# Writing each weight's low part in two halves: a one-core kernel for a hybrid decoder layer

## The chip, the core and the metric

The kernel runs on one core of one Trainium2 chip. The metric is the device time of one execution in microseconds (us). The core has a matrix engine (PE; its weight loads are shown as PEld), a vector engine (DVE), an activation engine (ACT), a general engine (POOL) and an engine that only issues transfers (SP). Each works through its own queue of instructions in order and waits for the others by semaphores.

## What is computed

One layer of a decoder, for a prompt of 1024 tokens and a sample group of 8 x 8 tokens with the same weights. Two branches read the same input: A, sparse attention, whose keys are the best 256 by a small indexer; B, gated linear attention (GLA) over four heads. Cut to what matters here:

```python
z = split_projection(x @ w_in)                 # q, k, v, indexer, GLA and gate columns
attn = attend(q_a, k_a, v_a, q_i, k_i, z['w_i'])      # top 256 keys by indexer score, softmax
log_a = log_sigmoid(z['a_b'] @ w_alpha2 + b_alpha) / GATE_TAU
o_b, s_new = gla_chunked(q_b, k_b, v_b, log_a, s0, chunk)
...
branch_a = attn @ w_attn_o
branch_b = o_b @ w_gla_o
merged = sigmoid(z['gate_a']) * branch_a + sigmoid(z['gate_b']) * branch_b
h = layer_norm(DN_ALPHA * x + merged @ w_out, ln1_g, ln1_b)
ff = square(relu(h @ w_ff1)) @ w_ff2
y = layer_norm(DN_ALPHA * h + ff, ln2_g, ln2_b)
```

## The kernel before

The 1024 prompt tokens and 64 sample tokens stand side by side as 1088 columns, cut into chunks of 384, 384 and 320. Products are taken in single precision out of two reduced parts: an operand is the sum of a high part (`h`, a rounding copy on ACT) and a low part (`l`, the rest, a subtraction), and `mm3` makes three matmuls of each product: high by high, high by low, low by high.

The program has two phases. `front` holds the projections, the GLA, the indexer with its search for the 256 best keys, the attention, the merge and the output projection; `back` holds the MLP and the sample group's attention. In `front` the list `jobs` gives the order in which the weights are used: indexer queries, keys and values, attention queries, then for each GLA head its query, key and value weights, and between these the `g` and gate weights, last the three output weights of the branches. Each job has one weight of 128 output columns, 8 x 128 rows, so a page of 128 x 1024; the value weights of the GLA (`wvb`) have 256 columns and take two pages, and those of `wao` are 128 x 512.

For a weight, `w_load` (L493) issues the transfer into a raw page `wr`. `w_split` (L504) takes the pages `wh` and `wl`, writes the high part on ACT and makes a task of the low part. `w_low` (L515) is that task: it waits until `wh` is there by the planner's estimate, then writes `wl = wr - wh` by `sub` (L443). `sub` puts it on POOL or DVE, whichever the planner thinks will be done first, with a bonus for POOL (`WLATE`, 4 us, in all but the first and the last jobs). `w_get` (L528), called when a job begins, splits the next job's weight and runs what is left of its own weight's tasks at once. The first two weights are split by other code at the start.

What sets the order of instructions is a planner that runs while the program is written. `Clock` keeps an estimated time for each engine and for each written range of a tile. The streams (`Stream`, generators that write instructions and yield what they need next) stand in a list in `Order`; `run` (L309) takes the first one in the list whose needs are met by the estimate at PE's present time, lets it write up to its next yield, and begins again at the head of the list. Tasks stand at the head, then the attention, the GLA, the searches, and at the end the main stream with the projections, which fills PE when nothing else is ready. A stream that yields an empty tuple is ready again at once. So any change in what is written, or in its estimated time, can move instructions of all streams on all engines.

The names of the prediction: `qz` casts and `qi` subtractions on DVE come from the indexer's queries, `psi` are its score matmuls and `sc` its accumulated scores; `ga`, `gb` and `jk`, `jkb` belong to two searches over the prompt's scores (bit by bit: a count, a comparison, a predicated copy, the next trial value), one counting on DVE and one on ACT; `ppr` is a small matmul of the search over the samples' scores. In the GLA, `S` is the state after a chunk, `Sm` the state scaled for the next chunk's matmul into `po`, `u` the scaled update out of `pu`, `gst` the samples' states and `us` their updates, `gv` the values, overwritten by the outputs.

## Time and profile before

| | |
|---|---|
| three runs | 2011.14, 2012.15, 2012.97 us (median 2012.15) |
| profiled execution, its own time | 2010.23 us |
| its span, first to last instruction | 2008.5 us |
| mean granted clock of PE | 0.996 |
| `wl` on POOL | 66 operations, 151.1 us, 2292 ns each |
| `wh` on ACT | 76 operations, 75.2 us, 997 ns each |
| PE waits up to 1060 us, longest | 2.6, 2.6, 2.4 and 1.8 us |
| moved by DMA | 260.30 MB, 130 GB/s |

The phase `front` takes PE until about 1060 us (the last `pwo` matmul with a `wl` starts at 1057.9), `back` the rest. A row of a group in the profile gives the line, the engine, the operation, what is written and read, the count, then the busy time and the mean of one in ns, then the idle time of the engine just before them and what ended it. Nearly every row has line L266, since a helper records each instruction; the names of the tiles tell them apart. A row of the timeline begins with the start and the length in us; what stands in brackets is the idle time just before it and what ended that. `x4` behind a row means four instructions in a row merged, and the length is then that of all four.

### The profile page before, as it was taken

To read this page: it belongs to the slowest core of one execution; us is meant where nothing else is said; L and a number is where in the kernel's file an instruction comes from. 1 tells how busy PE (TensorE), PEld (TensorE's weight loads), DVE (VectorE), ACT (ScalarE), POOL (GpSimd) and SP (SyncE) were. 2 spreads that over 40 slices of the span, in tenths; PEclk is the share of its full clock that TensorE was granted. 3 is DMA by queue.
4 is the path that set the end of the run, shared out by engine and by line. 5 is a ranking of instruction groups with operands and counts; after the bars stand their busy time and mean duration, and the time that the engine had idled before them with its cause. 6 is when DMAs were issued, how large, how long until landed. Compare 5 with 4: busy or idle time off the path is not lost.

```text
span 2008.5 us, 34410 instructions
## 1 busy us (share of the span) xinstructions
PE 1978.6 (99%) x12341; PEld 1914.4 (95%) x12341; DVE 1294.2 (64%) x2698; ACT 1140.2 (57%) x2239; POOL 762.2 (38%) x569
## 2 busy tenths in 40 slices
PE   9999999999999999999999999999999999999998
PEld 8888989998999999999999999999999999999998
DVE  7886978887655856661376557777674445576635
ACT  6688768796667556770124445555654333445544
POOL 5143232232411132122133325656565543454455
PEclk9999999999999999999999999999999999999998
DMA  9464302213132234273761144555452354145542
GB/s 330 187 210 133 129 22 85 81 32 115 38 107 84 77 105 138 76 225 130 255 216 53 54 122 144 151 158 160 131 173 79 96 163 142 48 150 162 185 151 90
DMA packets 185163, 260.30 MB, mean 130 GB/s; under 512 B 22160, under 2 KB 121488, under 8 KB 184992
## 3 DMA queue, kind: packets, MB, share of 16 engines
q1 hardware_dynamic: 177440, 232.67, 36.4%
q0 software_dynamic: 7552, 25.43, 4.2%
q8 instruction: 97, 1.59, 0.3%
q14 instruction: 74, 0.61, 0.1%
HBM read 208.52 MB, written 49.51 MB: 128 GB/s over the span
## 4 chain that ended last, share of the span: by engine, by line
PE 64%; DVE 3%; issue 2%; ACT 1%; POOL 1%; SPq 1%; DMA 0%; ACTq 0%; POOLq 0%; DVEq 0%
PE pf L266 33%; PE gate L266 8%; PE pmb L266 5%; PE pwo L266 4%; PE pma L266 2%; PE gb L266 2%; PE psq L266 2%; PE pov L266 2%; PE ppt L266 1%; PE pob L266 1%; PE psc L266 1%; DVE as L266 1%; PE pst L266 1%; SPq L266 1%; DVE w L266 0%
## 5 line engine op out<-in xcount | busy, mean ns | idle before, releaser
L266 PE MATMUL pf<-a,w 128*128 128x384 f32 (+1 forms) x2304 | 398.9, 329 | 3.2 <-POOL a L266 1.3
L266 PE MATMUL pf<-h,w 128*128 128x384 f32 (+1 forms) x2304 | 395.3, 329 | 0.0
L266 PEld LDWEIGHTS pf<-a,w 128*128 128x128 f32 x2304 | 379.7, 188 | 7.7 <-ACT a L266 2.1
L266 PEld LDWEIGHTS pf<-h,w 128*128 128x128 f32 x2304 | 380.4, 188 | 2.9
L266 POOL TENSOR_TENSOR wl<-wr,wh 128x1024 fp32r<-128x1024 f32 (+1 forms) x66 | 151.1, 2292 | 424.0 <-ACT wh L266 341.9
L266 POOL TENSOR_TENSOR w<-wr,w 128x512 fp32r<-128x512 f32 x135 | 191.4, 1426 | 128.5 <-ACT w L266 119.2
L266 ACT ACTIVATE w<-wr 128x512 fp32r<-128x512 f32 x256 | 148.0, 619 | 34.2 <-PE pf L266 18.4
L266 DVE TENSOR_TENSOR w<-wr,w 128x512 fp32r<-128x512 f32 x121 | 123.1, 1023 | 53.0 <-ACT w L266 51.6
L266 DVE TENSOR_TENSOR acc<-acc,pf 128x384 f32<-128x384 f32 (+1 forms) x152 | 81.3, 538 | 82.5 <-PE pf L266 81.9
L266 PE MATMUL gate<-xh,wh 128*128 128x384 f32 (+1 forms) x384 | 130.2, 339 | 0.0
L266 PE MATMUL gate<-xh,wl 128*128 128x384 f32 (+1 forms) x384 | 125.5, 327 | 0.0
L266 PE MATMUL gate<-xl,wh 128*128 128x384 f32 (+1 forms) x384 | 125.4, 327 | 0.0
L266 ACT ACTIVATE wh<-wr 128x1024 fp32r<-128x1024 f32 (+1 forms) x76 | 75.2, 997 | 82.7 <-PE pmb L266 57.9
L266 POOL TENSOR_TENSOR a<-fr,a 128x384 fp32r<-128x384 f32 (+1 forms) x52 | 50.7, 975 | 181.7 <-ACT a L266 179.0
L266 ACT ACTIVATE a<-fr 128x384 fp32r<-128x384 f32 (+1 forms) x96 | 48.7, 507 | 105.7 <-DVE fr L266 104.3
L266 DVE TENSOR_TENSOR fr<-fr,pf 128x384 f32<-128x384 f32 (+1 forms) x96 | 50.7, 529 | 72.7 <-ACT fr L266 72.1
L266 ACT ACTIVATE jkb<-sc,gb_f 128x896 int8<-128x896 f32 (+2 forms) x96 | 86.1, 897 | 19.9 <-DVE gb_f L266 17.3
L266 ACT ACTIVATE fr<-pf 128x384 f32<-128x384 f32 (+1 forms) x96 | 44.7, 465 | 81.2 <-PE pf L266 80.1
L266 DVE TENSOR_SCALAR_CACHE_REDUCE jk<-sc,ga_f 128x1024 int8<-128x1024 f32 (+2 forms) x96 | 88.4, 921 | 2.2
L266 DVE CUSTOM_DVE_ANT_0 pp<-psq,msk 128x512 f32<-128x512 f32 (+3 forms) x96 | 51.2, 553 | 47.8 <-PE psq L266 44.6
L266 PE MATMUL psv<-wh,xh 128*128 128x256 f32 x288 | 80.8, 285 | 0.0
L266 PE MATMUL psv<-wl,xh 128*128 128x256 f32 x288 | 80.3, 283 | 0.0
(532 smaller groups left out, 5138.3 us busy)
## 6 DMA issues: line engine op xcount, KB each, us to landing
wr<-wff SPq DMA_DIRECT2D x254, 256.0 KB
wr<-w SPq DMA_DIRECT2D x42, 512.0 KB
ckr<-kT SPq DMA_DIRECT2D x256, 64.0 KB
ga_s<-gate SPq DMA_DIRECT2D x16, 544.0 KB
ci_s<-cig SPq DMA_DIRECT2D x16, 512.0 KB
kir<-ci_s SPq DMA_DIRECT2D x16, 512.0 KB
mgp<-ga_s SPq DMA_DIRECT2D x16, 384.0 KB
qa_s<-qa SPq DMA_DIRECT2D x8, 544.0 KB
```

What stands on the lines that cost most here:

```text
L266: r = f(*a, **k)
```

## The change

`w_low` writes the low part by two operations, each of half the page's columns (the second dimension is the row tile, so a half is four of eight tiles, or two of four), and yields an empty tuple behind each, so that the planner looks for another stream between them. Engine and bonus are chosen for each half by itself; the bonus is computed once for both.

```diff
     def w_low(l, r, h):
         yield [f32(h)]
-        sub(l, r, f32(h), WLATE if 1 < state["job"] < mix_at - 1 else 0.0)
+        late = WLATE if 1 < state["job"] < mix_at - 1 else 0.0
+        m = r.shape[1] // 2
+        for s in (slice(0, m), slice(m, 2 * m)):
+            sub(l[:, s], r[:, s], f32(h[:, s]), late)
+            yield ()
```

The numbers of instructions change little beside this: POOL has 135 `wl` operations where it had 66, DVE 14 where it had 10 (three of the start in both), and a few evictions and scalings change between ACT and DVE. For 64 of the 73 weight pages both halves are on POOL, next to each other in its queue; for seven one half is on POOL and one on DVE, for two both on DVE. The matmuls are the same in number; their order changes between the indexer's scores and about the end of the gates, and from the merge of branch B on it is as before.

The queue of POOL in the first GLA head, before and with the change (`gat` a masked attention block, `gkz` the samples' keys, the two `wl` in a row a `wvb` weight's pages):

```order
L266 AFFINE_SELECT gat<-gat 128x512
L266 TENSOR_TENSOR wl_0_3057<-wr_0_2747,wh_0_3056 128x1024
L266 TENSOR_TENSOR gkz<-kts,brow 128x512
L266 AFFINE_SELECT gat<-gat 128x512
L266 TENSOR_TENSOR wl_0_3312<-wr_0_3052,wh_0_3311 128x1024
L266 TENSOR_TENSOR wl_1_3315<-wr_4_3054,wh_1_3314 128x1024
L266 TENSOR_TENSOR gkz<-kts,brow 128x512
```

```order
L266 AFFINE_SELECT gat<-gat 128x512
L266 TENSOR_TENSOR wl_0_3074<-wr_0_2768,wh_0_3073 128x512 x2
L266 TENSOR_TENSOR gkz<-kts,brow 128x512
L266 AFFINE_SELECT gat<-gat 128x512
L266 TENSOR_TENSOR wl_0_3340<-wr_0_3069,wh_0_3339 128x512 x2
L266 TENSOR_TENSOR wl_1_3343<-wr_4_3071,wh_1_3342 128x512 x2
L266 TENSOR_TENSOR gkz<-kts,brow 128x512
```

Each page's low part is now two operations side by side; the rest stands as it was.

The queue of DVE in the indexer's scores, where the prediction's place A is, before and with the change:

```order
L266 SCALAR_TENSOR_TENSOR sc_557<-r,wtok,sc_557 128x384
L266 SCALAR_TENSOR_TENSOR sc_556<-r,wtok,sc_556 128x512 x2
L266 CAST qz<-qi_568 64x4x8 x4
L266 SCALAR_TENSOR_TENSOR sc_559<-r,wtok,sc_559 128x384
L266 TENSOR_TENSOR qi_832<-qi_0_834,qi_832 64x384
L266 TENSOR_TENSOR qi_833<-qi_0_834,qi_833 64x384
L266 SCALAR_TENSOR_TENSOR sc_560<-r,wtok,sc_560 128x512
```

```order
L266 SCALAR_TENSOR_TENSOR sc_558<-r,wtok,sc_558 128x384
L266 SCALAR_TENSOR_TENSOR sc_557<-r,wtok,sc_557 128x512 x2
L266 TENSOR_TENSOR qi_831<-qi_0_833,qi_831 64x384
L266 CAST qz<-qi_569 64x4x8 x4
L266 TENSOR_TENSOR qi_832<-qi_0_833,qi_832 64x384
L266 SCALAR_TENSOR_TENSOR sc_560<-r,wtok,sc_560 128x384
L266 SCALAR_TENSOR_TENSOR sc_561<-r,wtok,sc_561 128x512
```

One `qi` subtraction moved ahead of the casts, and the `sc` update moved behind both subtractions.

The queue of DVE from one `S` to the next in the first GLA head, place B, before and with the change:

```order
L266 TENSOR_SCALAR us<-pus,gsc_2910 128x256
L266 SCALAR_TENSOR_TENSOR gst_3092<-gst_3092,gsc_2910,us 128x256
L266 TENSOR_SCALAR ga_m<-ga_n 128x3
L266 COPY_PREDICATED ga_u<-ga_m,ga_f 128x3
L266 TENSOR_SCALAR ga_f<-ga_u 128x3
L266 TENSOR_SCALAR jk,ga_n<-sc_556,ga_f 128x1024
L266 SCALAR_TENSOR_TENSOR gst_3092<-gst_3092,gsc_2910,us 128x256
L266 SCALAR_TENSOR_TENSOR S<-S,gsc_2910,u 128x256
```

```order
L266 TENSOR_SCALAR ga_m<-ga_n 128x3
L266 COPY_PREDICATED ga_u<-ga_m,ga_f 128x3
L266 TENSOR_SCALAR ga_f<-ga_u 128x3
L266 TENSOR_SCALAR jk,ga_n<-sc_557,ga_f 128x1024
L266 COPY gv_2782<-po 128x256
L266 TENSOR_SCALAR us<-pus,gsc_2952 128x256
L266 SCALAR_TENSOR_TENSOR gst_3102<-gst_3102,gsc_2952,us 128x256
L266 TENSOR_TENSOR gb_m<-gb_n,gb_l 128x3
L266 COPY_PREDICATED gb_u<-gb_m,gb_f 128x3
L266 TENSOR_SCALAR gb_f<-gb_u 128x3
L266 SCALAR_TENSOR_TENSOR gst_3102<-gst_3102,gsc_2952,us 128x256
L266 SCALAR_TENSOR_TENSOR S<-S,gsc_2952,u 128x256
```

The `gv`, `us` and three `gb` operations now stand between the count and `S`. The queue of ACT at the same place, before and with the change (`gv,gss` is a square with its sum, `wh_0` and `wh_1` the `wvb` weight's high parts):

```order
L266 ACTIVATE jkb,gb_n<-sc_560,gb_f 128x512
L266 ACTIVATE gq_3059<-qb_2_3236 128x320
L266 ACTIVATE wh_0_3311<-wr_0_3052 128x1024
L266 ACTIVATE wh_1_3314<-wr_4_3054 128x1024
L266 ACTIVATE Sm<-S,gsc_2910 128x256
```

```order
L266 ACTIVATE Sm<-S,gsc_2952 128x256
L266 ACTIVATE gv_2782,gss_3085<-po 128x256
L266 ACTIVATE u<-pu,gsc_2952 128x256
L266 ACTIVATE jkb,gb_n<-sc_558,gb_f 128x896
L266 ACTIVATE jkb,gb_n<-sc_559,gb_f 128x768
L266 ACTIVATE gq_3076<-qb_2_3287 128x320
L266 ACTIVATE wh_0_3339<-wr_0_3069 128x1024
L266 ACTIVATE wh_1_3342<-wr_4_3071 128x1024
L266 ACTIVATE gv_2782,gss_3085<-po 128x256
L266 ACTIVATE jkb,gb_n<-sc_561,gb_f 128x512
L266 ACTIVATE gk_3345<-kb_0_3346 128x384
L266 ACTIVATE Sm<-S,gsc_2952 128x256
```

`Sm` stood directly behind the two high parts; now a square, a count and a copy of `gk` stand between. On PE, the `qb` and `kb` matmuls between this `Sm`'s matmul and the one before it are 24 instead of 30.

## The prediction

> **What bounds the kernel now.** I read the page's table of busy time first, then windows over the span, then what PE waited for, then the timeline at the longest of these waits.

> ```profile
> PE 1978.6 (99%) x12341; PEld 1914.4 (95%) x12341; DVE 1294.2 (64%) x2698; ACT 1140.2 (57%) x2239; POOL 762.2 (38%) x569
> 0.00:100.00 100.00, 94.25 (x528) 87.94 (x529) 82.02 (x183) 65.77 (x137) 37.00 (x38) 0.98 0.71 260
> 400.00:500.00 100.00, 97.42 (x646) 91.58 (x645) 78.51 (x199) 79.47 (x167) 27.27 (x14) 0.98 0.22 72
> 800.00:900.00 100.00, 100.00 (x678) 98.66 (x677) 64.52 (x199) 77.57 (x166) 21.47 (x17) 1.00 0.46 140
> ```

> The columns of a window are its length, the busy time of PE, PEld, DVE, ACT and POOL, then the granted clock, the DMA share and GB/s. PE is the bound: 1978.6 of 2008.5 us, so only 29.9 us of the span are PE's idle time. Neither the number of matmuls nor their shapes change. All that a change of POOL and DVE work can do is to move these idle us and the stretches at a lower clock, and only in the front, whose weights the edited helper splits; after about 890 us, at the 800:900 row, the front's PE is full. The idle time that can be reached is in the first 600 us:

> ```profile
> PE po L266 <- ACT Sm L266: 2.9, 2, 2.6
> PE psi L266 <- DVE qi L266: 2.7, 2, 2.4
> PE ppr L266 <- ACT u L266: 2.6, 1, 2.6
> PE qi L266 <- DVE wl L266: 0.4, 1, 0.4
> ```

> The numbers are total, times and longest, in us. Only the last row waits for a low part itself, and it belongs to one of the two weights of the start, which other code splits and the change leaves alone. So the low parts are in time; what they cost must be indirect, through DVE. That is visible:

> ```profile
> 290.43 4.87 POOL L266 TENSOR_TENSOR wl<-wr,wh 128x1024 fp32r<-128x1024 f32 x2 [8.00 <-ACT wh L266]
> 288.77 0.48 DVE L266 SCALAR_TENSOR_TENSOR gst<-gst,gsc,us 128x256 f32<-128x256 f32 x1
> 290.97 2.13 DVE L266 SCALAR_TENSOR_TENSOR gst<-gst,gsc,us 128x256 f32<-128x256 f32 x1
> 293.02 2.56 DVE L266 SCALAR_TENSOR_TENSOR S<-S,gsc,u 128x256 f32<-128x256 f32 x1
> 295.62 0.51 ACT L266 ACTIVATE Sm<-S,gsc 128x256 f32<-128x256 f32 x1 [4.32 <-DVE S L266]
> 296.18 0.70 PE L266 MATMUL po<-Sm,gq 128*128 128x256 f32 x2 [2.62 <-ACT Sm L266]
> ```

> The same `gst` update takes 0.48 us alone and 2.13 us while POOL writes a low part, `S` 2.56; each ends 0.2 to 0.3 us after one POOL operation of 2.4 us. DVE is held for the whole POOL operation and gets one operation through between two of them. `S` feeds `Sm` on ACT, `Sm` feeds PE, PE idles 2.62 us. This is what shorter POOL operations act on.

> **The sum, part by part.** The sum is made against the profiled execution: 2010.23 us, of which 2008.5 are the span and 1.73 lie around it. The median of the three runs is 2012.15, 1.92 above it, and I add that at the end.

> *The operation itself.*

> ```profile
> L266 POOL TENSOR_TENSOR wl<-wr,wh 128x512 fp32r<-128x512 f32 x7 | 9.1, 1294 | 27.1 <-ACT wh L266 15.7 <-DVE mg L266 8.5 <-issue 2.9
> L266 POOL TENSOR_TENSOR wl<-wr,wh 128x1024 fp32r<-128x1024 f32 x50 | 121.6, 2435 | 328.5 <-ACT wh L266 289.3 <-issue 28.5 <-DMA ci_s<-cig 5.1
> ```

> Two halves cost 2 x 1.294 = 2.59 us against 2.435, so 0.15 us more per weight, and some 50 x 0.15 = 7.5 us of POOL in the first 900. POOL is busy 27 and 21 of 100 us in the windows above and no PE row waits for a low part there, so I count it as nothing; without that cover it would be 0.15 us at each of 50 weights. The halves read and write the same bytes and no DMA is added; a raw page comes free one half later at most, and no PE wait in the front ends on a DMA.

> *Place A, near 70 us.* PE waits for a PSUM bank that DVE's `qi` subtractions free.

> ```profile
> 60.01 2.39 POOL L266 TENSOR_TENSOR wl<-wr,wh 128x1024 fp32r<-128x1024 f32 x1 [7.86 <-ACT wh L266]
> 60.85 2.16 DVE L266 CAST qz<-qi 64x32 fp32r<-64x32 f32 x4
> 68.85 0.75 DVE L266 CAST qz<-qi 64x32 fp32r<-64x32 f32 x4
> 69.63 0.62 DVE L266 SCALAR_TENSOR_TENSOR sc<-r,wtok,sc 128x384 f32<-128x384 f32 x1
> 70.28 1.14 DVE L266 TENSOR_TENSOR qi<-qi,qi 64x384 fp32r<-64x384 f32 x2
> 71.57 0.47 PE L266 MATMUL psi<-kkh,qi 128*128 128x512 f32 x1 [2.41 <-DVE qi L266]
> 72.00:73.00 1.00, 1.00 (x7) 0.87 (x6) 1.00 (x3) 0.64 (x2) 0.00 (x0) 0.92 1.00 250
> 74.00:75.00 1.00, 1.00 (x5) 1.00 (x4) 1.00 (x3) 0.99 (x3) 0.00 (x0) 0.50 0.99 406
> ```

> Four casts that take 0.75 us took 2.16 behind a low part, and DVE then had no idle time until the subtractions. Halving the low part lets two casts through instead of one, 0.19 us, and the low part is 0.15 longer: nothing gained. But the order moves here (the DVE rows in the section on the change): the `sc` update of 0.62 us now stands behind both subtractions. They end 0.62 us earlier and the wait falls to about 1.8 us, since the PE rows ahead of it are the same in number. Behind the gap the granted clock was 0.50 for over 3 us (0.92, three windows near 0.50, then 0.87: 1.7 us lost). A nearby gap bears on what is left of it:

> ```profile
> 270.97 0.70 PE L266 MATMUL pu<-gv,gkt 128*128 128x256 f32 x2 [1.76 <-ACT gkt L266]
> 272.00:273.00 1.00, 1.00 (x8) 1.00 (x7) 0.00 (x0) 0.97 (x4) 1.00 (x1) 1.00 0.00 0
> ```

> After 1.76 us of waiting the clock stayed at 1.00. So A lies between -0.6 (the drop stays) and -2.3 (it goes); being next to the 1.76 row, I take **-2.3**. [...]

> *Place B, near 296 us.* In the changed order `S` stands beside the four halves of the same two-page weight. I count from the end of the `S` before it.

> ```profile
> 284.69 0.49 DVE L266 SCALAR_TENSOR_TENSOR S<-S,gsc,u 128x256 f32<-128x256 f32 x1 [0.32 <-ACT u L266]
> 288.04 0.42 DVE L266 COPY gv<-po 128x256 f32<-128x256 f32 x1 [1.14 <-ACT gv L266]
> 289.16 0.17 DVE L266 TENSOR_SCALAR ga_m<-ga_n 128x3 int32<-128x3 f32 x1
> 289.77 1.28 DVE L266 TENSOR_SCALAR_CACHE_REDUCE jk<-sc,ga_f 128x1024 int8<-128x1024 f32 x1
> 285.46 1.04 ACT L266 ACTIVATE jkb<-sc,gb_f 128x896 int8<-128x896 f32 x1
> 289.28 2.01 ACT L266 ACTIVATE wh<-wr 128x1024 fp32r<-128x1024 f32 x2
> 569.86 4.28 PE gb L266 x24
> ```

> On DVE the new order has six operations on three columns (0.2 us each from start to start), a count (1.28) and five of 256 columns (0.4 to 0.5), `S` the last: 4.4 us. On ACT the `wh` copy that releases POOL comes behind `Sm`, a square, `u`, two counts and `gq`: with 0.4 to 0.5 us for each small one, 1.1 and 0.9 for the counts and 1.0 for the copy, 4.8, so POOL starts near 4.9. `S` is done half a microsecond before the halves begin. But `Sm` on ACT now stands behind both `wh` copies, a square, a count and a `gk` copy, and ends near 8.0. PE has 24 filler matmuls there instead of 30 (24 of this kind take 4.28 us) and arrives near 6.0: a wait of 2.0 us. I take **-0.6**. The bounds are -2.6 (the wait goes) and +4.0: `S` is held by all four halves, from 4.9 to 10.1, `Sm` ends near 10.9, PE waits 4.9 us and loses 1.7 more at the low clock, as at A.

> *Place C, near 465 us.*

> ```profile
> 455.60 2.38 POOL L266 TENSOR_TENSOR wl<-wr,wh 128x1024 fp32r<-128x1024 f32 x1 [4.54 <-ACT wh L266]
> 455.63 2.38 DVE L266 COPY_PREDICATED gb_u<-gb_m,gb_f 128x3 int32<-128x3 int32 x1
> 465.30 0.34 PE L266 MATMUL ppr<-gs_p,pm 128*128 128x2 f32 x1 [2.58 <-ACT u L266]
> 467.00:468.00 1.00, 1.00 (x9) 0.35 (x2) 0.97 (x4) 0.96 (x4) 0.00 (x0) 0.50 0.28 103
> ```

> Here a chain of two DVE operations stands in the way of the search on ACT. With halves, `gb_u` gets through after 1.3 us, but the next half then holds `gb_f` for another 1.3: 2.59 in all against 2.38. The mechanism gives nothing, the new order may give up to the wait and the low clock behind it (2.6 + 1.7, as at A): from -4.3 to +0.2; I take 0.

> *The streams that move elsewhere* (matmuls of other streams and evictions of PSUM change places up to 890 us) can lose as well as gain; the bounds are the waits seen so far, 2.6 us each, to either side, and I take 0. The work of the back, from the first `pf` matmul on, stands in the same order.

> Sum: -2.3 - 0.6 + 0 + 0 = -2.9 us: 2007.3 on the scale of the profiled execution, 2009.2 on that of the median. Forecast **2009 us**.

> **Rivals.** *The gaps move and add up to the same.* For it: the order is new over 800 us, and a planner that works with its own estimates has no reason to leave less idle time than before. Against it: DVE is held for at most 1.3 us at a time. It gives 2012.

> *All three gaps close.* Then -2.3 - 2.6 - 4.3 = -9.2: 2003. For it: each of the three has a held DVE operation behind it. Against: A and C are chains, which two adjacent halves hold as long as one whole.

> *Slower: `S` falls behind the halves.* Place B decides, by half a microsecond between 4.4 on DVE and 4.9 on POOL. If DVE is that much later, `S` goes through the halves behind the `gst` and `gb` operations, one per half, and B costs +4.0. Head 0 alone, with A at -2.3, gives 2013.9, no change that can be measured. The same two-page weight comes again:

> ```profile
> 394.95 4.75 POOL L266 TENSOR_TENSOR wl<-wr,wh 128x1024 fp32r<-128x1024 f32 x2 [10.59 <-ACT wh L266]
> 380.00:400.00 20.00, 20.00 (x127) 19.13 (x126) 16.84 (x48) 16.38 (x37) 5.79 (x3) 1.00 0.36 121
> ```

> From the second such head on, where no gap was before, it costs 4.9 + 1.7 = 6.6 more: 2020.5. Against it: before the change PE was busy for the whole 20 us around that second one, so its `S` has room.

> *The change does not do what it says.* In the new order the halves of 64 of 73 weights stand side by side on POOL, with nothing between them. [...] If POOL went on with its second half before a waiting DVE operation, DVE would be held 2.59 us instead of 2.44 and nothing would be won: 2012 to 2013. The rows at 290 us speak against it, since `gst` got through between two adjacent POOL operations.

> **How the numbers follow.** Forecast 0.40, the same in other places 0.22, all gaps closed 0.13, slower 0.20, no effect 0.05. A measurement of this kernel tells a difference of about 0.2%, 4 us, from none. The forecast lies 3 us below, so about half of its chance is under 2008.1: faster 0.20 + 0.13 = 0.33. Slower is the third rival, 0.20; the rest, 0.47, is within 0.2%. The range goes from the closed gaps, 2003, to 2017, between one held head and two; half of the slower case and part of the closed gaps lie outside.

> **What would show it.** PE's wait for `qi` near 70 us: 1.8 us, with the clock at 1.00 behind it. `gst` and `S` during a low part: at most about 1.5 us each instead of 2.1 to 2.6. PE's wait for `Sm` in head 0: near 2 us, 0 if the closed gaps are right, near 5 if `S` is held. Low parts in POOL's groups: 1.29 us a half, some 0.15 us more per weight. PE's busy time within 2 us of 1978.6. The prediction is wrong if waits of over 2 us stand at new places, if PE comes to wait for `wl`, or if its busy time moves, which nothing here foresees.

## The result, and the profile with the change

| | before | with the change |
|---|---|---|
| median of five runs each, same chip | 2011.8 us (2010.37 to 2012.97) | 2001.32 us (2000.21 to 2003.4) |
| profiled execution, its own time | 2010.23 us | 2002.63 us |
| its span | 2008.5 us | 2000.9 us |
| PE idle from 16 to 1060 us | 13.35 us | 7.27 us |
| lost there to a low granted clock | 3.41 us | 1.71 us |
| `wl` on POOL | 66 operations, 151.1 us | 135 operations, 171.4 us |

The ratio is 0.995 (95% interval 0.9939 to 0.9961): 10.5 us faster, where 2.9 were forecast; the time lies below the forecast's range. The two rows on idle time and clock are sums over windows of 1 us: what PE was not busy, and one less the granted clock wherever that is under 0.97. (In the kernel before, the last `pwo` matmul with a `wl` starts at 1089.3 us, not at 1057.9; but from 1060 to 1095 us PE is never idle in either kernel.) Together they fall by 7.8 us, and the spans differ by 7.6, so in the profiled executions the whole gain is accounted for. (The medians differ by 2.9 us more than these two executions do; how much of the low clock there is changes from one execution to the next, as the last section shows.)

The page's table of busy time, windows over the span, and four rows of what PE waited for up to 1060 us, with the change:

```profile
PE 1977.4 (99%) x12341; PEld 1914.6 (96%) x12341; DVE 1288.1 (64%) x2704; ACT 1132.7 (57%) x2235; POOL 781.1 (39%) x640
0.00:100.00 100.00, 95.08 (x523) 88.32 (x524) 83.68 (x182) 65.00 (x136) 38.23 (x42) 0.98 0.71 260
400.00:500.00 100.00, 98.56 (x659) 93.35 (x659) 72.55 (x185) 85.35 (x177) 31.32 (x26) 1.00 0.23 77
800.00:900.00 100.00, 100.00 (x665) 98.89 (x664) 58.32 (x175) 68.05 (x150) 25.71 (x25) 1.00 0.48 151
PE psi L266 <- DVE qi L266: 2.1, 2, 1.8
PE ppr L266 <- ACT jka L266: 1.9, 4, 0.6
PE qi L266 <- DVE wl L266: 0.6, 1, 0.6
PE po L266 <- ACT Sm L266: 0.5, 2, 0.3
```

PE's busy time hardly moved, and the last window was full before. Of the three waits of over 2 us one is left, at 1.8; those for `Sm` (2.6) and `u` (2.6) are gone, and a fourth, of 1.76 us for `gkt`, which stood outside the forecast's sum, is gone too. Small waits for `jka` are new. As before, the one wait for a low part itself (0.6 us) belongs to a weight of the start.

Place A, with the change: PE and DVE in the timeline, and a window of 1 us behind the gap.

```profile
72.42 0.77 PE L266 MATMUL psi<-kkh,qi 128*128 128x512 f32 x1 [1.81 <-DVE qi L266]
70.38 0.55 DVE L266 TENSOR_TENSOR qi<-qi,qi 64x384 fp32r<-64x384 f32 x1
70.94 0.74 DVE L266 CAST qz<-qi 64x32 fp32r<-64x32 f32 x4
71.71 0.56 DVE L266 TENSOR_TENSOR qi<-qi,qi 64x384 fp32r<-64x384 f32 x1
73.00:74.00 1.00, 1.00 (x4) 0.91 (x3) 1.00 (x2) 0.70 (x2) 0.00 (x0) 0.50 0.84 213
```

The wait is the 1.8 us that the moved `sc` update gave. The low clock behind it is still there.

Place B, with the change: DVE, POOL and PE in the first GLA head.

```profile
284.02 0.48 DVE L266 SCALAR_TENSOR_TENSOR S<-S,gsc,u 128x256 f32<-128x256 f32 x1
289.28 0.48 DVE L266 SCALAR_TENSOR_TENSOR S<-S,gsc,u 128x256 f32<-128x256 f32 x1
291.72 0.35 DVE L266 TENSOR_SCALAR Sm<-S,gsc 128x256 f32<-128x256 f32 x1
292.62 5.22 POOL L266 TENSOR_TENSOR wl<-wr,wh 128x512 fp32r<-128x512 f32 x4 [10.66 <-ACT wh L266]
294.22 0.48 DVE L266 TENSOR_SCALAR u<-pu,gsc 128x256 f32<-128x256 f32 x1
294.73 0.71 DVE L266 SCALAR_TENSOR_TENSOR S<-S,gsc,u 128x256 f32<-128x256 f32 x1
295.36 1.25 DVE L266 TENSOR_TENSOR gb_m<-gb_n,gb_l 128x3 int32<-128x3 f32 x1
296.64 1.22 DVE L266 COPY_PREDICATED gb_u<-gb_m,gb_f 128x3 int32<-128x3 int32 x1
295.47 0.51 ACT L266 ACTIVATE Sm<-S,gsc 128x256 f32<-128x256 f32 x1 [0.55 <-DVE S L266]
292.64 0.60 PE L266 MATMUL po<-Sm,gq 128*128 128x256 f32 x2
```

`S` is done 2.9 us before the halves begin, `Sm` of this chunk is written on DVE, and PE does not wait. What the halves hold now are `gb` operations, and PE has no idle time from 288 to 304 us. One of the two `gb` operations passes for each half, in 1.25 and 1.22 us. Not every DVE operation is held: `u`, which reads the matmul's result `pu`, took its usual 0.48 us in the middle of the halves.

Place C, with the change: the search's matmul, the low part, and what it holds on DVE.

```profile
460.69 0.35 PE L266 MATMUL ppr<-gs_p,pm 128*128 128x2 f32 x1
452.73 2.72 POOL L266 TENSOR_TENSOR wl<-wr,wh 128x512 fp32r<-128x512 f32 x2 [0.97 <-ACT wh L266]
452.77 1.53 DVE L266 SCALAR_TENSOR_TENSOR S<-S,gsc,u 128x256 f32<-128x256 f32 x1
```

The low part falls on another operation than before, and neither the wait of 2.58 us nor the low clock behind it is there.

### The profile page after: what moved, and what is told of

Same layout as the page of the kernel before. It is cut to its first block, busy times and chain, and to the rows that moved or that the text cites. A ratio compares the mean times of both kernels' runs of the same rounds, so it can differ in the third digit from the quotient of the medians.

```text
span 2000.9 us, 34496 instructions
## 1 busy us (share of the span) xinstructions
PE 1977.4 (99%) x12341; PEld 1914.6 (96%) x12341; DVE 1288.1 (64%) x2704; ACT 1132.7 (57%) x2235; POOL 781.1 (39%) x640
## 4 chain that ended last, share of the span: by engine, by line
PE 64%; DVE 3%; ACT 2%; issue 2%; POOL 1%; DMA 1%; SPq 0%; ACTq 0%; POOLq 0%; DVEq 0%
PE pf L266 32%; PE gate L266 8%; PE pwo L266 5%; PE pmb L266 5%; PE gb L266 2%; PE pma L266 2%; PE psq L266 2%; PE pov L266 2%; PE ppt L266 2%; PE pob L266 1%; PE psc L266 1%; DVE as L266 1%; PE pst L266 1%; POOL w L266 0%; SPq L266 0%
## 5 line engine op out<-in xcount | busy, mean ns | idle before, releaser
L266 PE MATMUL pf<-a,w 128*128 128x384 f32 (+1 forms) x2304 | 398.6, 329 | 3.3 <-POOL a L266 1.3
L266 PE MATMUL pf<-h,w 128*128 128x384 f32 (+1 forms) x2304 | 395.2, 329 | 0.0
L266 PEld LDWEIGHTS pf<-a,w 128*128 128x128 f32 x2304 | 379.4, 188 | 7.8 <-ACT a L266 2.2
L266 PEld LDWEIGHTS pf<-h,w 128*128 128x128 f32 x2304 | 380.3, 188 | 2.9
L266 POOL TENSOR_TENSOR wl<-wr,wh 128x512 fp32r<-128x512 f32 (+1 forms) x135 | 171.4, 1291 | 405.1 <-ACT wh L266 319.3
L266 POOL TENSOR_TENSOR w<-wr,w 128x512 fp32r<-128x512 f32 x135 | 191.9, 1430 | 127.4 <-ACT w L266 118.4
L266 ACT ACTIVATE w<-wr 128x512 fp32r<-128x512 f32 x256 | 147.7, 619 | 34.1 <-PE pf L266 18.2
L266 DVE TENSOR_TENSOR w<-wr,w 128x512 fp32r<-128x512 f32 x121 | 124.4, 1033 | 51.8 <-ACT w L266 50.4
L266 DVE TENSOR_TENSOR acc<-acc,pf 128x384 f32<-128x384 f32 (+1 forms) x152 | 81.3, 538 | 82.1 <-PE pf L266 81.5
L266 PE MATMUL gate<-xh,wh 128*128 128x384 f32 (+1 forms) x384 | 130.1, 339 | 0.0
L266 PE MATMUL gate<-xh,wl 128*128 128x384 f32 (+1 forms) x384 | 125.6, 327 | 0.0
L266 PE MATMUL gate<-xl,wh 128*128 128x384 f32 (+1 forms) x384 | 125.6, 327 | 0.0
L266 POOL TENSOR_TENSOR a<-fr,a 128x384 fp32r<-128x384 f32 (+1 forms) x52 | 50.7, 976 | 181.4 <-ACT a L266 175.6
L266 ACT ACTIVATE wh<-wr 128x1024 fp32r<-128x1024 f32 (+1 forms) x76 | 75.2, 995 | 78.7 <-PE pmb L266 55.4
L266 ACT ACTIVATE a<-fr 128x384 fp32r<-128x384 f32 (+1 forms) x96 | 48.7, 507 | 105.8 <-DVE fr L266 105.8
L266 DVE TENSOR_TENSOR fr<-fr,pf 128x384 f32<-128x384 f32 (+1 forms) x96 | 50.7, 529 | 74.8 <-ACT fr L266 74.0
L266 ACT ACTIVATE jkb<-sc,gb_f 128x896 int8<-128x896 f32 (+2 forms) x96 | 86.1, 897 | 15.5 <-DVE gb_f L266 14.2
L266 ACT ACTIVATE fr<-pf 128x384 f32<-128x384 f32 (+1 forms) x96 | 44.6, 465 | 81.0 <-PE pf L266 79.9
L266 DVE TENSOR_SCALAR_CACHE_REDUCE jk<-sc,ga_f 128x1024 int8<-128x1024 f32 (+2 forms) x96 | 88.4, 921 | 2.2
L266 DVE CUSTOM_DVE_ANT_0 pp<-psq,msk 128x512 f32<-128x512 f32 (+3 forms) x96 | 51.2, 553 | 52.0 <-PE psq L266 45.4
L266 PE MATMUL psv<-wh,xh 128*128 128x256 f32 x288 | 80.8, 285 | 0.0
L266 PE MATMUL psv<-wl,xh 128*128 128x256 f32 x288 | 80.3, 283 | 0.0
```

Of the source, the lines that this page charges most:

```text
L266: r = f(*a, **k)
```

## Experiments: the operation and the order, each alone

The change does two things: the operation on the chip is shorter, and the planner, which now counts two shorter operations for one, draws another order of all streams. **Theory:** the shorter operation ("hold") brings the gain. **Rival:** the order brings it. Two kernels separate them. In both, `pick` chooses the engine by the rule of `sub`, `plan` tells the planner of an operation and `write` writes one without telling it. The first keeps the order of before: the planner is told of one operation, and two halves are written.

```diff
-        sub(l, r, f32(h), WLATE if 1 < state["job"] < mix_at - 1 else 0.0)
+        late = WLATE if 1 < state["job"] < mix_at - 1 else 0.0
+        m = r.shape[1] // 2
+        e = pick(l, late)
+        plan(e, l, r, f32(h))
+        for s in (slice(0, m), slice(m, 2 * m)):
+            write(e, l[:, s], r[:, s], f32(h[:, s]))
```

> The order of before on all engines, planned as before; only on the chip each low part is two operations of half the columns on the engine that had the whole. If the shorter hold of DVE makes the gain (theory H): most of the 10.5 us, 2002 to 2006 beside 2012, with PE's wait for Sm near 296 us under 1 us. If the new order makes it (theory O): 2010 to 2013, with the three gaps of before (qi, Sm, ppr) still there within 1 us each.

The second keeps the order of the change: the planner is told of two halves, and one operation is written where both are on one engine (for seven weights they are not, and there the halves stay).

```diff
+        done = []
         for s in (slice(0, m), slice(m, 2 * m)):
-            sub(l[:, s], r[:, s], f32(h[:, s]), late)
+            e = pick(l[:, s], late)
+            plan(e, l[:, s], r[:, s], f32(h[:, s]))
+            done.append((e, s))
+            if len(done) == 2:
+                if done[0][0] is e:
+                    write(e, l, r, f32(h))
+                else:
+                    for x, p in done:
+                        write(x, l[:, p], r[:, p], f32(h[:, p]))
             yield ()
```

> The order of after on all engines, planned with two halves; on the chip each low part whose halves share an engine is one whole operation, written where the second half stood (seven weights with a half on each engine keep their halves). Theory H: the gain goes, 2008 to 2012. Theory O: it stays, 2000 to 2003, and DVE operations of 2.1 to 2.6 us beside the low parts are there again without PE waiting for them.

Measured: halves in the old order 2006.76 us (ratio 0.9978, 0.9969 to 0.9987), whole operations in the new order 2004.14 us (0.9962, 0.9948 to 0.9975). Against the kernel before on the same chip that is -4.9 and -7.6 us, and both together -10.5. Both times lie between what the theory and the rival gave, so each part is real; which is the larger is not shown, since the intervals of the two ratios overlap.

PE's idle time from 16 to 1060 us gives no ranking either: 13.35 us before, 10.90 with halves in the old order, 10.79 with whole operations in the new one, 7.27 with both. Each part alone takes away 2.5 us of waits; the low clock, 3.41 us before, took 0 and 1.71 us in these two executions. With whole operations in the new order PE waits longer than with halves for `gv` (1.6 for 0.5 us), `gk` (1.6 for 0.3) and `wsf` (1.1 for 0.4). Apart from the `wl` operations, each of the two kernels runs PE, DVE, ACT and POOL in the sequence of the kernel whose order it keeps.

The timeline of the first, halves in the old order, shows what the hold does at the three places and at the fourth:

```profile
72.39 0.47 PE L266 MATMUL psi<-kkh,qi 128*128 128x512 f32 x1 [2.38 <-DVE qi L266]
74.00:75.00 1.00, 1.00 (x8) 1.00 (x7) 1.00 (x3) 1.00 (x3) 0.00 (x0) 1.00 0.97 365
239.09 1.60 DVE L266 TENSOR_SCALAR cu<-psa,b_al 128x384 f32<-128x384 f32 x3 [1.71 <-ACT ge L266]
288.22 1.03 DVE L266 SCALAR_TENSOR_TENSOR gst<-gst,gsc,us 128x256 f32<-128x256 f32 x1
289.18 1.50 DVE L266 SCALAR_TENSOR_TENSOR S<-S,gsc,u 128x256 f32<-128x256 f32 x1
291.28 0.70 PE L266 MATMUL po<-Sm,gq 128*128 128x256 f32 x2 [0.47 <-ACT Sm L266]
453.35 1.21 DVE L266 TENSOR_SCALAR gb_f<-gb_u 128x3 int32<-128x3 int32 x1
461.66 0.27 PE L266 MATMUL ppr<-gs_p,pm 128*128 128x2 f32 x1 [2.52 <-ACT u L266]
```

At A nothing changes (2.38 for 2.41), and yet there is no low clock behind this gap. At B `S` takes 1.50 us instead of 2.56, and PE's wait there falls from 2.62 to 0.47 (a wait for another `Sm`, of 1.2 us, is new). At C the second operation of the chain, `gb_f`, is held by the second half, and the wait stays (2.52 for 2.58). The fourth place is in the row of `cu`, the start of the gates' chain in the GLA, at whose end stands `gkt`. In the kernel before, the timeline has at that place:

```profile
239.95 2.41 POOL L266 TENSOR_TENSOR wl<-wr,wh 128x1024 fp32r<-128x1024 f32 x1 [7.53 <-issue]
240.11 2.28 DVE L266 TENSOR_SCALAR ga_f<-ga_u 128x3 int32<-128x3 int32 x1
242.42 1.60 DVE L266 TENSOR_SCALAR cu<-psa,b_al 128x384 f32<-128x384 f32 x3
```

`ga_f`, an operation on three columns (0.17 us in the median of 32), was held for 2.28 us with `cu` behind it in DVE's queue; with halves DVE is early instead and waits 1.71 us for ACT. The whole chain from `cu` (242.42 before, 239.09 now) to `gkt` (270.32 and 266.98) runs 3.3 us earlier, and PE's wait for `gkt` is gone.

## Experiments: quarters

If one DVE operation passes for each POOL operation, quarters should shorten the holds again. First quarters that the planner knows of, in an order of their own, then quarters at the two orders that are already measured:

```diff
-        m = r.shape[1] // 2
-        for s in (slice(0, m), slice(m, 2 * m)):
+        m = r.shape[1] // 4
+        for s in (slice(i * m, i * m + m) for i in range(4)):
```

> Each low part by four operations of a quarter of the columns, planned so; the order changes again. Theory H: a further gain of 1 to 4 us on after, 1997 to 2000, since a DVE operation is held for 0.75 us at most. Theory O: a new draw, anywhere from 1998 to 2013, with no relation to the length of the operations.

> Order of the kernel before, each low part written by four operations of a quarter of the columns; the planner still counts one. Theory 'hold': a GpSimd operation lets VectorE in only at its end, so what a low part costs the other streams goes with the length of one operation. From 2.435 us (1024 columns) and 1.294 us (512) one of 256 columns is worked out at 0.72 us. Cutting 2.44 to 1.29 gave -4.9 us at this order; in proportion, 1.29 to 0.72 gives another -2.4 us: 2004.4, and at least 2003 to 2006. Rival 'count': the start of each operation (0.15 us, 132 more of them, 20 us on GpSimd in all) comes into the path: above the halves' 2006.8, 2008 to 2012. Rival 'saturated': the waits left in that run (2.4 and 2.5 us) are of other causes, 2006 to 2007.5.

For the order of the change, each half that the planner knows of is written by two operations of a quarter:

```diff
-            sub(l[:, s], r[:, s], f32(h[:, s]), late)
+            e = pick(l[:, s], late)
+            plan(e, l[:, s], r[:, s], f32(h[:, s]))
+            q = s.start + m // 2
+            for p in (slice(s.start, q), slice(q, s.stop)):
+                write(e, l[:, p], r[:, p], f32(h[:, p]))
```

> Order of the changed kernel, each planned half written by two operations of a quarter of the columns. Theory 'hold': the waits that one operation of a half still lends to VectorE shorten again; in the old order the second halving gave -5.2 us (2006.8 to 2001.55), but the changed kernel has only 7.3 us of TensorE idle before 1060 us left against 10.9 there, and its largest waits (1.81 for qi, 1.4 for kir) stand in orders that shorter operations have not moved: -1 to -3 us, 1998.5 to 2000.5, below both kernels. Rival 'used up': what is left of the waits is the order's, 2001 to 2002. Rival 'count': the starts of 135 more operations (0.15 us each) reach the path, 2003 or more.

Measured: 2000.27 us (ratio 0.9943, 0.9928 to 0.9959), 2001.55 us (0.9952, 0.9938 to 0.9965) and 1999.46 us (0.994, 0.9926 to 0.9953). In the old order the second halving gives nearly as much again as the first (2011.06, the kernel before on that chip; -4.9 with halves; -9.5 with quarters), more than the proportion said (2001.55 for 2003 to 2006), and no cost of the count of operations shows. The quarters in their own order, 2000.27, do not tell the hold from a new draw, which reached from 1998 to 2013. In the order of the change the quarters' -12.2 us stand against -10.5: the lowest time of this study, below the kernel before beyond doubt, but the intervals of the two ratios overlap, so not surely below the change. The timeline of quarters in the old order:

```profile
288.25 6.15 POOL L524 TENSOR_TENSOR wl<-wr,wh 128x256 fp32r<-128x256 f32 x8 [8.00 <-ACT wh L266]
289.19 0.96 DVE L266 SCALAR_TENSOR_TENSOR S<-S,gsc,u 128x256 f32<-128x256 f32 x1
290.08 0.69 DVE L266 TENSOR_TENSOR gb_m<-gb_n,gb_l 128x3 int32<-128x3 f32 x1
290.80 0.65 DVE L266 COPY_PREDICATED gb_u<-gb_m,gb_f 128x3 int32<-128x3 int32 x1
451.00 0.66 DVE L266 TENSOR_SCALAR gb_f<-gb_u 128x3 int32<-128x3 int32 x1
458.82 0.27 PE L266 MATMUL ppr<-gs_p,pm 128*128 128x2 f32 x1 [1.47 <-ACT u L266]
```

A small operation on DVE, 0.17 us alone, takes 2.3 us, 1.2 and 0.65 as POOL writes whole parts, halves and quarters. At place C the chain of two passes after two quarters, and PE's wait falls by 1.1 us: what halves could not do there.

## Experiments: other orders

Is the order's part a property of the change, or a draw? The planner adds an allowance to each engine's estimated end; a hair more or less of it gives another order from the same rules. Both kernels were run with three other allowances:

```diff
-LAG = 0.3
+LAG = 0.29
```

> Whole low parts, but the planner's allowance for a hand-over between engines is 0.29 us instead of 0.30, so the order is drawn anew with nothing else changed. If the new order's share of the gain was luck of the draw: anywhere from 2004 to 2016, and not always above the kernel with halves and the same allowance. If planning with halves is what makes the better order: 2009 to 2014.

> Halves as in the change, allowance 0.29 us. Luck of the draw: 1999 to 2011, on average some 3 to 5 us (the shorter hold) below the whole ones. Planning with halves makes it: 1999 to 2004, like the change.

> Whole low parts, allowance 0.305 us: a second draw. Luck of the draw: 2004 to 2016. Planning with halves makes it: 2009 to 2014.

> Halves as in the change, allowance 0.305 us. Luck of the draw: 1999 to 2011. Planning with halves makes it: 1999 to 2004.

> Kernel before with the planner's allowance at 0.295 us in place of 0.3, which draws another order. Theory 'halving and a draw': the order alone moves whole operations over 2011.7 to 2020.8 so far; another time in 2008 to 2021, and the halves at the same allowance below it by 5 to 10 us. Rival 'a draw only': the two stand in either order, with a difference anywhere in -8 to +8 us.

> Changed kernel with the planner's allowance at 0.295 us. Theory 'halving and a draw': 2001 to 2015, below the whole operations at the same allowance by 5 to 10 us (so far -10.5, -10.5 and -5.5). Rival 'a draw only': above or within 2 us of them.

At 0.29 and 0.305 the changed kernel was below the whole operations, as at 0.3. At 0.295 it was 7.6 us above, against what was expected. That planning with halves makes the better order is out: 2006.56 and 2015.31 lie outside its 1999 to 2004, 2017.10 and 2020.79 outside its 2009 to 2014 for whole operations. The draws also spread wider than was expected of them, which was up to 2016. That left open whether halves can cost time, and five kernels crossed operation and order, by the two edits of the first section at these allowances:

> Order of the changed kernel with the allowance at 0.29 (2006.56), the two halves of a weight written as one operation where both are on one engine. Theory 'hold': the longer operation costs what it did in the other two orders, 2.8 to 4.9 us: 2009.4 to 2011.5; the rest up to the whole operations at 0.29 (2017.1) is the order. Rival 'order alone': within 1 us of 2006.6. Rival 'hold alone': 2015 to 2017, as the whole operations in their own order.

> Order of the changed kernel with the allowance at 0.295 (2018.99), whole operations. Theory 'hold and order apart': whole operations cost 1.5 to 5 us more than halves in this order too, 2020.5 to 2024, and the order alone makes the changed kernel slower here. Rival 'no gain in this order': 2018 to 2020. Rival 'halves are what costs here': below 2017, towards the whole operations' 2011.4.

> Order of the changed kernel with the allowance at 0.305 (2015.31), whole operations. Theory 'hold and order apart': 2017 to 2020. Rival 'no gain in this order': 2014.5 to 2016.

> Order of the whole operations with the allowance at 0.295 (2011.39), each written as two halves. Theory 'hold and order apart': 2 to 5 us below, 2006.5 to 2009.5. Rival 'no gain in this order': 2010.5 to 2012.5.

> Order of the whole operations with the allowance at 0.29 (2017.1), each written as two halves. Its largest wait, 6.0 us of TensorE for Sm from VectorE, would shrink by the hold alone. Theory 'hold and order apart': 2 to 6 us below, 2011 to 2015. Rival 'no gain in this order': 2016 to 2018. Rival 'hold alone': near the changed kernel's 2006.6.

All medians, as the difference in us from the kernel before on the same chip (2011.06 to 2012.14; each ratio's interval reaches 0.0009 to 0.0017 to either side, so 2 to 3.4 us):

| allowance | whole, its own order | halves, the whole operations' order | whole, the halves' order | halves, their own order |
|---|---|---|---|---|
| 0.3 | 0 | -4.9 | -7.6 | -10.5 |
| 0.29 | +5.5 | +4.8 | -2.6 | -5.1 |
| 0.295 | +0.3 | -5.1 | +12.5 | +7.9 |
| 0.305 | +9.2 | not run | +6.5 | +3.7 |

The hold, from a whole operation to halves at one order (out of the unrounded medians): -4.9, -0.7, -5.5 and -2.9, -2.4, -4.6, -2.8 us, a mean of -3.4, and a loss in none of the seven. Each difference hangs on two intervals, so those under 3 us are not shown one by one. PE's idle time up to 1060 us fell by 2.5 to 3.5 us in five of the seven pairs, but not in the two at 0.29 (10.68 to 10.73 and 16.03 to 17.81 us). The order, at whole operations: -7.6, -8.1, +12.2, -2.6, so either sign, with a mean of -1.5 from four draws. Rival "halves are what costs" at 0.295 is out: whole operations are slower still in that order. Its largest wait, in the timelines of halves and (last row) whole operations in that order:

```profile
427.41 2.29 DVE L266 TENSOR_TENSOR_SCAN sc<-one,gta 128x1024 f32<-128x1024 f32 x1
429.74 2.38 DVE L266 SCALAR_TENSOR_TENSOR gta<-sc,cg,gta 128x1024 int8<-128x1024 f32 x1
432.04 2.35 DVE L266 TENSOR_TENSOR gk<-gk,cu 128x1088 f32<-128x1088 f32 x1
434.53 0.30 PE L266 MATMUL psas<-gq,gk 128*64 128x64 f32 x2 [4.21 <-DVE gk L266]
```

```profile
437.13 0.44 PE L266 MATMUL psas<-gq,gk 128*64 128x64 f32 x2 [4.18 <-DVE gk L266]
```

The planner put a scan and other long operations of a search ahead of `gk`, for which PE waits 4.2 us either way. The hold is part of it both times: two halves hold the `gta` update and `gk` for 1.1 us each (they take 1.28 and 1.27 us where POOL does not hold them), one whole operation holds `gk` alone, which then takes 3.43 us. In the changed kernel at 0.3 the two stand the other way round:

```profile
424.13 1.27 DVE L266 TENSOR_TENSOR gk<-gk,cu 128x1088 f32<-128x1088 f32 x1
425.33 3.25 DVE L266 TENSOR_TENSOR_SCAN sc<-one,gta 128x1024 f32<-128x1024 f32 x1
```

Where the order puts a chain of DVE operations beside the low parts, halves bring little, as at place C (2.58 to 2.52 us). At 0.29 in the whole operations' order (2016.91 us, so the rival "no gain in this order" held), PE waits for an `Sm` on DVE, first with whole operations, then with halves:

```profile
PE po L266 <- DVE Sm L266: 6.0, 1, 6.0
286.10 2.65 DVE L266 SCALAR_TENSOR_TENSOR S<-S,gsc,u 128x256 f32<-128x256 f32 x1
288.67 2.29 DVE L266 TENSOR_TENSOR gb_m<-gb_n,gb_l 128x3 int32<-128x3 f32 x1
```

```profile
PE po L266 <- DVE Sm L266: 5.9, 1, 5.9
287.59 1.57 DVE L266 SCALAR_TENSOR_TENSOR S<-S,gsc,u 128x256 f32<-128x256 f32 x1
289.08 1.21 DVE L266 TENSOR_TENSOR gb_m<-gb_n,gb_l 128x3 int32<-128x3 f32 x1
```

Three `gb` operations stand between `S` and `Sm`. Two whole operations hold `S` and `gb_m` for over 2 us each; four halves hold `S` and all three `gb` operations, 1.2 to 1.6 us each, and `gkz` behind them holds `Sm` (1.21 us). So this wait is a hold in both, and the way of the prediction's slower rival, the `gb` operations passing one per half with PE waiting at the end, does occur in another order.

## Why the prediction was wrong

Term by term, as taken and as the two profiled executions gave it: place A -2.3, measured -0.6; place B -0.6, measured -2.6; place C 0, measured -4.3; the rest 0, measured -1.8 at `gkt` and +1.5 of new small waits. Together -2.9 was taken and -7.8 measured. The mechanism was right; the terms failed, each for its own reason.

**What acts.** Right: DVE is held for a whole POOL operation, 2.3, 1.2 and 0.65 us beside wholes, halves and quarters (not in every operation: `u` at place B, 0.48 us, is one that is not held), and gets one through between two, adjacent ones too, so the rival that nothing would be won by two neighbouring halves is out. The rows also show who comes next: a waiting DVE operation, even when POOL has another ready. Before, `gst` ended at 293.10 us, 0.3 us after the first of two adjacent whole operations (292.82) and 2.2 us ahead of the end of the second (295.30).

**The operation itself.** Right that it is hidden: no PE wait for a low part is new. With 135 halves for 67.5 weights it is 171.4 / 67.5 - 151.1 / 66 = 0.25 us more per weight, not 0.15.

**Place A.** The wait was right, 1.81 for 1.8, and so was its cause: 2.38 us with halves in the old order, and 1.8 with whole operations in the new one. Wrong was the step to -2.3, "being next to the 1.76 row", by which the low clock would go: it stayed, and A gave -0.6. A gap's length does not decide it here: 1.81 us was followed by 0.50, and 2.38 us at the same place, with halves in the old order, by 1.00. In the traces, as the last section shows, the clock went with how much idle time fell into one window of 3.41 us (1.65 us with the change, 1.04 and 1.34 with halves in the old order), and where the windows lay at A was luck.

**Place B.** Taken at -0.6, it gave its bound, -2.6. The step that failed is "`Sm` on ACT now stands behind both `wh` copies": that `Sm` (295.47) reads the next `S` (294.73). The one for this chunk was on DVE (291.72), outside the rows that are shown ahead of the result. The count of times also failed: from the end of the `S` before it, 284.50, `S` ended after 5.3 us, not 4.4, and the halves began after 8.1, not 4.9, since I had added up durations and left out waits between the engines (DVE 0.99 us for ACT's `gv`, ACT 1.45 us for DVE's `gb_f`). That is also why the slower rival, decided by half a microsecond, did not come: `S` had 2.9 us to spare.

**Place C.** The largest single miss: taken at 0, it gave its bound of -4.3, wait and low clock. "The mechanism gives nothing" was right (2.52 us with halves in the old order); "the new order may give up to the wait" was the term that was set to 0 without a reason, since the new queue was not followed there as it was at A and B. The order took the wait away.

**What was not in the sum.** The wait for `gkt`, 1.76 us, served in the prediction only as a reading of the clock, though it is the fourth longest of PE's waits before. It was the end of a hold 30 us earlier, `ga_f` ahead of `cu`, that the sum does not follow. Together: -0.6 - 2.6 - 1.8 - 2.6 of waits, +1.5 of new small ones, -1.7 of low clock: -7.8.

**The moved streams.** The error of the range. They were taken at 0, with bounds of 2.6 us to either side. Zero is a fair centre (the mean of four draws is -1.5), but the draws reach from -8.1 to +12.2. The sum followed the new order at three places and nowhere else, and its range was that of those places; with the order's spread it would have had to reach some 8 us below the forecast and 12 above, and 2001.3 would just have been in it. The hold alone, -2.9 to -4.9 at the two orders of this case, is near the -2.9 that was forecast, but only by chance: that sum put most of it at A, where the hold does nothing.

## What to carry to other kernels

Where traces show one engine held for the whole of another's operation, as DVE was here by POOL (2.3 us beside wholes, 1.2 beside halves, 0.65 beside quarters), the length of the side job's operation is a latency for the held engine's queue, even if neither is full (POOL 38% busy before, DVE 64%): cut it, and look upstream of each wait, not only at the last operation before it. When an edit also feeds a planner, measure the edit at a fixed order (tell the planner the old thing, write the new one) before crediting it; here the order alone moved whole operations by -8 to +12 us, and the halves gained 3.4 us, the mean of seven pairs. A few redraws of the order by a harmless constant show that spread, and it belongs in the range.

## What the hardware showed that was not expected

In all eighteen traces, from 16 to 1980 us, the clock goes with PE's idle time in each such window: behind all 27 windows at full clock with more than 1.70 us of it the clock fell, and behind none of the more than 10000 with less than 1.62; of the three between, 1.65 and 1.69 had a drop and another 1.69 had none. That is about half a window. (What comes after 1980 us is left out: there PE runs matmuls of a single column, and the clock falls although the profile shows PE busy, at 1997.96 us in the kernel before.) Of the gap of 2.41 us at A, 2.14 lay in one window, of 2.58 at C all, and the window of the 1.81 with the change holds 1.65 us of idle time. The three without a drop were cut by the grid, 2.38 into 1.04 and 1.34 us, 2.52 into 1.03 and 1.49, 2.62 into 1.15 and 1.47, and the window of the 1.76 us for `gkt` held 1.61.

In the longest gap (whole operations, allowance 0.29) the clock fell while PE still waited, and it did not come back with the first matmuls but over 3 us later. Windows of 1 us there, from 286.5 us on without work for PE:

```profile
288.00:289.00 1.00, 0.00 (x0) 0.00 (x0) 1.00 (x2) 0.00 (x0) 1.00 (x2) 0.86 0.00 0
292.00:293.00 1.00, 0.52 (x1) 0.50 (x2) 1.00 (x4) 0.74 (x1) 0.00 (x0) 0.50 0.00 0
295.00:296.00 1.00, 1.00 (x5) 1.00 (x5) 0.57 (x4) 0.30 (x2) 0.00 (x0) 0.73 0.00 0
```

A gap is thus dearer by about 1.7 us when it meets a drop. From these figures, an estimate: a lone gap under about 1.65 us is safe, one over about 3.3 us always brings a drop, since the grid can cut it only in two (the four of 4.18 to 5.95 us each had one), and between these the place of the grid decides, which the order of this kernel does not set. It shows in the spread of one kernel's executions: with halves in the old order they go from 2005.06 us at a mean granted clock of 0.998 to 2010.32 us at 0.995.
